# Hybrid Mamba-2 and attention layer on one core: operand splits get an edge behind the copies of turned blocks, and two half-size products change places

## The chip, the cores and the metric

One core of a Trainium2 chip runs the whole layer in one launch. The metric is device time in microseconds (us). The engines are TensorE (PE, with PEld for its weight loads), VectorE (DVE), ScalarE (ACT), GpSimd (POOL) and SyncE (SP, which here issues DMAs). ScalarE's queue issues DMAs too (ACTq).

## The reference

Input is x of 1024 x 1024, float32. One layer is computed:

```python
h = rmsnorm(x, pre_g)
proj = h @ w_in     # -> z_ssm | xBC | dt | q | k | v | f | z_att | g_ssm | g_att
# A: Mamba-2: causal conv and SiLU on xBC, chunked SSD scan, norm gated with silu(z_ssm)
# B: forgetting attention, 16 heads of 64: softmax(q k^T / 8 + F[t] - F[s]), causal,
#    F = cumsum(log_sigmoid(f)); output times silu(z_att)
merged = sigmoid(g_ssm) * (y_ssm @ w_branch_ssm) + sigmoid(g_att) * (y_att @ w_branch_att)
out = x + rmsnorm(merged @ w_out, post_g)
```

The result is compared with float32, so the kernel multiplies float32 values as sums of a high and a low part.

## The kernel before

**Products.** The projections are done in pairs of column blocks of 128 (`Pair`). A pair is a 2 x 2 block product done with seven half-size products instead of eight (Strassen's scheme), numbered 1 to 7. Each has an operand made of the weights (`a11`, `a12`, `a21`, `a22` or sums of them) and one made of the activations (`ops`). An operand is used as a high part, which ScalarE makes by a copy to a narrower type (`Pair.split`, L351, tile `wop`), and a low part, which VectorE makes as the difference (L352). A product is 12 matmuls of 128x512 in L130: four blocks of 128 rows times high x high, high x low, low x high. In the rows of the profile `x0h`, `x4h`, `x5h` are the activations' parts, so `x0` marks product 1, `x4` product 6, `x5` product 7.

Products 1, 6, 7 and 4 of a pair accumulate in one PSUM bank (`pb`), which ScalarE copies out between them (`keep`, L404); 5 and 3 accumulate in a second (`pc`), and 2 has a third. `give` (L412 to L418) adds what belongs together and hands it to the unit's handler, which applies gates and stores to DRAM.

**The stream.** `Stream.steps` is a list, written out by hand, of all products in the order in which TensorE runs them. `half()` issues half of the next product. With it, the operand of the product three steps ahead is prepared (`ahead`, `prepare`), and up to two splits of activations are made for pairs that use another operand set (`ops.some()`, L277 and L280). There are four `wop` tiles.

**Attention.** The loop at the end makes 48 visits (eight pairs of heads, six groups of query blocks each) and a last pass. A visit issues, in this order: the scores of two query blocks (`scores`: products into PSUM tiles `s`, then VectorE's addition of the bias and minimum at L1467, then ScalarE's exponential at L1471, tile `ex`); the weighted sums of the visit before (`weighted`, tile `av`); a number of halves of the stream (`ahead`); loads; the turning of the exponentials (`turned`: transposes on TensorE into tiles `pt`, copied to `p` by ScalarE at L1510, or by VectorE at L1508 for one block in four); and more halves (`behind`). `s` and `pt` share four PSUM banks, so that a copy `p<-pt` must end before the scores of the next visit can use its bank. Between `hold()` and `release()` the calls of `ops.some()` are put off to the next visit. `ends[4]` is the pair whose products run when the attention loop ends.

**Order.** A planner in the framework orders the instructions on each engine by priority and by dependences. What is traced in `tc.high_priority()` (the copies, `keep`, `give`, the exponentials) goes ahead of other work that is ready. `tc.issue_after(ins)` gives the instructions traced inside it an edge: on the engine of `ins` they come after it in the queue.

Of the kernel before, what the change touches and what calls it, by code (L numbers as in the profile page):

```python
# [11 lines left out]
AF = mybir.ActivationFunctionType  # L12
# [74 lines left out]
def hybrid_layer(ctx: ExitStack, tc, a, out):  # L87

    nc = tc.nc
# [42 lines left out]
    def turn(out_, in_, idn=ident):  # L132
        return tc.keep_in_program_order(nc.tensor.transpose(out_, in_, idn))  # L133
# [27 lines left out]
    class Operands:  # L161
# [9 lines left out]
        def __init__(self, name, src, there=lambda k, h: True, order=lambda op: op, queue=nc.gpsimd):  # L171
            self.src, self.there, self.order, self.queue = src, there, order, queue
            self.copy = src
            self.tiles, self.left, self.made, self.at, self.step = {}, {}, set(), {}, 0
            self.lows = {}
            self.dram = {n: tc.dram_tile([KH, P, HALF], F32, name=f"{n}_{name}") for n in self.LESS}
# [279 lines left out]
    class Stream:  # L456
# [6 lines left out]
        def __init__(self, pairs, double, last):  # L463
            self.pairs = pairs
            for n, p in enumerate(pairs):
                p.bank, p.other = (pj, "be"[n % 2]), (pjx, "d") if n < double else (pj, "c")

                p.between = n < double or n >= last

            p, q, r = pairs[0:3]  # L470
            self.steps = [(p, 1), (q, 1), (p, 2), (q, 2)] + [(p, n) for n in (6, 5, 7, 4, 3)]
            self.steps += [(q, 6), (q, 5), (q, 7), (r, 1), (q, 4), (q, 3)]
            for n in range(2, last):
                p, nxt = pairs[n], pairs[n + 1]
                self.steps += [(p, i) for i in ((2, 6, 5, 7) if n < double else (6, 2, 7, 5))] + [(nxt, 1)]
                self.steps += [(p, 4), (p, 3)] if n + 1 < last else [(p, 3), (p, 4)]

            a, b, c, d, e, f, g, h = pairs[last:]
            self.steps += [(a, 5), (a, 6), (a, 7), (b, 1), (a, 2), (a, 4), (a, 3)]
            for p, nxt in ((b, c), (c, d), (d, e)):  # L480
                self.steps += [(p, 2), (p, 6), (p, 5), (p, 7), (nxt, 1), (p, 4), (p, 3)]
            self.steps += [(f, 1), (e, 2), (e, 6), (e, 5), (e, 7), (f, 2), (e, 4), (e, 3)]
            self.steps += [(f, 6), (f, 5), (f, 7), (g, 1), (f, 4), (f, 3)]
            self.steps += [(g, 2), (g, 6), (g, 5), (g, 7), (h, 1), (g, 4), (g, 3)]
            self.steps += [(h, 6), (h, 5), (h, 7), (h, 2), (h, 3), (h, 4)]
            self.following = {p: n.ops for p, n in zip(pairs, pairs[1:]) if n.ops is not p.ops}
            self.building = []
            self.chores, self.line = [], []
            self.held = None
            self.count = 0  # L490
            self.at = 0
            self.run = None
            self.waiting = []
            self.loads = [(p, names) for p in pairs for names in (("a11", "a12"), ("a21", "a22"))]
            self.loaded = []
            self.load_next()
# [23 lines left out]
                self.prepare(p, which)  # L520

        def prepare(self, p, which):
            p.prepare(which)
            self.load_more()

        def after(self, halves, fn):

            self.waiting.append([halves, fn])

        def half(self):  # L530
            if self.run is None:
                if self.at == len(self.steps):
                    return False
                p, which = self.steps[self.at]
                if which == 7 and p.ops is ops_a and "merged" not in fin:
                    return False
                if p.ops is ops_a and not all(p.ops.ready(OPERAND[which].strip("-"), j) for j in range(KH)):
                    return False
                self.ahead(False)
                for ops in self.building:  # L540
                    ops.some(OPERAND[which])
                self.run = p.do(which)
                next(self.run)
            else:
                for _ in self.run:
                    pass
                self.run = None
                p, which = self.steps[self.at]
                if p in self.following:
                    ops = self.following[p]  # L550
                    if ops not in self.building:
                        self.building.append(ops)
                    ops.open(OPERAND[which])
                self.ahead(True)
                self.at += 1
            for ops in self.building:
                if self.held is None:
                    ops.some()
                else:
                    self.held.append(ops)  # L560
            for chores in (self.chores, self.line):
                if chores:
                    chore = chores.pop(0)
                    if chore:
                        chore()
            self.count += 1
            for w in self.waiting:
                w[0] -= 1
            for w in [w for w in self.waiting if w[0] <= 0]:
                self.waiting.remove(w)  # L570
                w[1]()
            return True
# [4 lines left out]

        def release(self):
            held, self.held = self.held or [], None
            for ops in held:  # L580
                ops.some()

        def do_chores(self):
            while self.chores:
# [550 lines left out]
    with tc.tile_pool(name="pro", bufs=1, reuse_waits="tile", side="right") as pro, tc.tile_pool(  # L1135
# [37 lines left out]
        def turned(tiles, k):  # L1173
            pt = prop.tile([P, HALF], F32, tag="pt", bufs=2, name="pt")
            for j in range(4):
                turn(pt[:, j * P : (j + 1) * P], tiles[j][:, k * P : (k + 1) * P]) 
            return pt
# [11 lines left out]
        stream = Stream(order + late + ends, len(order) + 3, len(order) + len(late) + 4)  # L1189
# [105 lines left out]
    with tc.tile_pool(name="att", bufs=1, reuse_waits="tile", side="right") as ap, tc.tile_pool(  # L1295
# [177 lines left out]
        def turned(hp, g, sent):  # L1473

            pair, h = GROUPS[g]
            bs = list(range(4 * h, min(4 * h + 4, pair[0] + 1)))
            made = {}  # L1480
            order = bs[-1:] + bs[:-1] if sent else bs
            tiles = {b: pp.tile([P, HALF], F32, tag="s", bufs=4, name="pt") for b in order}
            banks = {b: tiles[b].rearrange("p (e t c) -> p e t c", e=2, t=2) for b in order}

            def turn_one(b, e, t):
                turn(banks[b][:, e, t, :], ex[:, e, 1 - t, b % 4 * P : b % 4 * P + P])

            for e in range(2):
                for b in order:
                    turn_one(b, e, 1)  # L1490
            for b in order:
                bank, first = banks[b], max(b - pair[1], 0)
                if sent and b == bs[-1]:
                    assert first == 1
                    for hd, which in sent:
                        hd.turn(which, tiles[b])
                if not first:
                    for e in range(2):
                        turn_one(b, e, 0)
                if sent and b == bs[-1]:  # L1500
                    for hd, which in sent:
                        hd.send(which, tiles[b])
                p = ap.tile([P, 2, 2, P], F32, tag="p", bufs=4, name="p")
                to, src = (x[:, :, first:, :] for x in (p, bank))
                with tc.high_priority():

                    if b % 4 == 1 and hp < NK - 2:
                        nc.vector.tensor_copy(to, src)  # L1508
                    else:
                        nc.scalar.activation(to, src, AF.Copy)  # L1510
                made[b] = (hp, g, b, first, p)
            return [(*made[b], b == bs[0], b == bs[-1]) for b in bs]

# [116 lines left out]
        def room(m):  # L1630

            share = weights[m // 6] * rooms[m % 6] if m < 6 * NK - 1 else 1.4
            to = stream.steps.index((ends[4], 6))
            n = round((2 * (to - stream.at) - (stream.run is not None)) * share / left[0])
            left[0] -= share
            if m == 6 * NK - 1:
                return n // 2, n - n // 2
            behind = n // 2 if n > 3 else min(max(n - 1, 0), 1)
            return n - behind, behind

        made = []
        for m in range(6 * NK + 1):
# [9 lines left out]
            for hd, which in end(m - 1):  # L1652
                hd.free(which)
            if m == 6 * NK:
                stream.release()
                heads[NK - 1].out(2)
                break
# [9 lines left out]
            ahead, behind = room(m)  # L1667
# [82 lines left out]
```

## Time and profile before

| | us |
|---|---|
| median of the runs | 1289.23 |
| lowest of the runs | 1288.09 |
| profiled execution, its own time | 1288.76 |
| span of the profiled execution | 1287.0 |
| TensorE busy in it | 1253.9 |
| VectorE busy | 1010.0 |
| ScalarE busy | 794.7 |
| GpSimd busy | 259.8 |

The mean granted clock of TensorE was 0.997. The attention loop lies between about 690 and 1135 us from the start of the span; the projections of the merged branches and the output follow. A row of the timeline gives start, duration, engine, line, operation, output tile <- input tiles, shapes and count, and in brackets the idle time of the engine ahead of it with what ended it. A matmul's duration overlaps with the next one's, so the distance of two starts is the time that one takes from TensorE.

### The profile page before, as it was taken

Reading aid. Unit: us, or ns where it says so; the run is one execution under the profiler, and the core shown is the slowest. Engines: PE = TensorE matmul, PEld = TensorE weight load, DVE = VectorE, ACT = ScalarE, POOL = GpSimd, SP = SyncE. Lnnn points to the kernel's source line nnn. Section 1 sums busy time; section 2 is a strip of 40 time slices with the busy share of each in tenths; the row PEclk is TensorE's granted clock in tenths of the full one; section 3 lists DMA queues with packets and bytes.
Section 4 is the critical chain, followed back from the end, with each engine's and each line's share of the span. In section 5 each row is a group of like instructions: output and inputs, shape, how many; then the busy total and the mean of one; then the engine's idle time right before and its main releaser. Section 6 shows DMA issues by size and latency. Waiting matters only on the chain.

```text
span 1287.0 us, 20996 instructions
## 1 busy us (share of the span) xinstructions
PE 1253.9 (97%) x7054; PEld 987.4 (77%) x7054; DVE 1010.0 (78%) x1994; ACT 794.7 (62%) x1738; POOL 259.8 (20%) x250
## 2 busy tenths in 40 slices
PE   5999999999999999999999999999989999999997
PEld 4688888787888888878877777777767777778886
DVE  7988886987788978897767676767679666897976
ACT  7745665556665665566556666666667665753754
POOL 4000440013300330124101111211000111246052
PEclk9999999999999999999999999999999999999999
DMA  8232542646336533653356566665787656765932
GB/s 298 70 116 76 158 150 88 191 151 189 127 115 198 185 126 106 213 168 123 132 185 233 178 212 200 206 225 202 237 285 244 206 184 224 258 229 194 365 115 98
DMA packets 153515, 233.57 MB, mean 181 GB/s; under 512 B 15968, under 2 KB 61504, under 8 KB 153408
## 3 DMA queue, kind: packets, MB, share of 16 engines
q1 hardware_dynamic: 137408, 197.14, 47.4%
q10 hardware_dynamic: 11136, 19.11, 3.9%
q0 software_dynamic: 4864, 15.99, 3.2%
q8 instruction: 55, 0.90, 0.3%
q14 instruction: 52, 0.43, 0.1%
HBM read 162.99 MB, written 72.34 MB: 183 GB/s over the span
## 4 chain that ended last, share of the span: by engine, by line
PE 73%; DVE 9%; DMA 8%; ACT 5%; issue 3%; SPq 1%; POOL 0%; ACTq 0%; DVEq 0%; POOLq 0%
PE pb L130 30%; PE pc L130 17%; PE pd L130 6%; PE av L130 5%; PE s L130 5%; PE pt L133 5%; PE yps L130 2%; DVE wop L352 2%; DMA raw<-in_wu 1%; DVE sum L357 1%; DMA xt<-in_x 1%; PE st L130 1%; DVE xs L771 1%; PE tr L133 1%; ACT wop L351 1%
## 5 line engine op out<-in xcount | busy, mean ns | idle before, releaser
L352 DVE TENSOR_TENSOR wop<-sum,wop 128x512 fp32r<-128x512 f32 x180 | 138.6, 772 | 54.6 <-ACT wop L351 53.7
L351 ACT ACTIVATE wop<-sum 128x512 fp32r<-128x512 f32 x180 | 112.5, 626 | 111.5 <-DVE sum L357 52.8
L1471 ACT ACTIVATE ex<-ex,nm 128x512 f32<-128x512 f32 (+1 forms) x192 | 116.2, 606 | 71.8 <-DVE nm L1467 67.7
L404 ACT ACTIVATE s<-pb 128x512 f32<-128x512 f32 x144 | 85.1, 591 | 98.3 <-PE pb L130 95.3
L130 PE MATMUL pb<-x0h,wop 128*128 128x512 f32 x384 | 131.8, 400 | 0.0
L130 PE MATMUL pc<-x2h,wop 128*128 128x512 f32 x384 | 131.1, 400 | 0.3 <-DVE u L416 0.3
L130 PE MATMUL pc<-x3h,wop 128*128 128x512 f32 x384 | 129.8, 396 | 1.5 <-DVE th L414 1.2
L130 PE MATMUL pb<-x5h,wop 128*128 128x512 f32 x384 | 130.0, 395 | 1.0 <-ACT s L404 1.0
L130 PE MATMUL pb<-x6h,wop 128*128 128x512 f32 x384 | 129.5, 395 | 1.3 <-ACT s L404 1.3
L352 DVE TENSOR_TENSOR wop<-raw,wop 128x512 fp32r<-128x512 f32 x144 | 102.7, 714 | 34.4 <-ACT wop L351 33.7
L130 PE MATMUL pb<-x4h,wop 128*128 128x512 f32 x384 | 129.1, 395 | 0.0
L1467 DVE CUSTOM_DVE_ANT_0 ex<-s,fb 128x512 f32<-128x512 f32 (+1 forms) x192 | 96.9, 552 | 17.9 <-PE s L130 17.9
L351 ACT ACTIVATE wop<-raw 128x512 fp32r<-128x512 f32 x144 | 89.7, 623 | 13.1 <-PE pd L130 5.8
L130 PE MATMUL pd<-x1h,wop 128*128 128x512 f32 x288 | 96.3, 394 | 0.0
L130 PEld LDWEIGHTS pc<-x2h,wop 128*128 128x128 f32 x384 | 72.6, 189 | 18.0 <-issue 2.4
L130 PEld LDWEIGHTS pc<-x3h,wop 128*128 128x128 f32 x384 | 72.1, 188 | 18.7 <-DVE th L414 1.6
L130 PEld LDWEIGHTS pb<-x5h,wop 128*128 128x128 f32 x384 | 72.1, 188 | 18.6 <-ACT s L404 2.1
L130 PEld LDWEIGHTS pb<-x6h,wop 128*128 128x128 f32 x384 | 72.1, 188 | 18.5 <-issue 2.0
L130 PEld LDWEIGHTS pb<-x0h,wop 128*128 128x128 f32 x384 | 72.8, 189 | 17.6 <-issue 2.9
L130 PEld LDWEIGHTS pb<-x4h,wop 128*128 128x128 f32 x384 | 72.1, 188 | 16.7 <-issue 1.9
L133 PE MATMUL pt<-ident,ex 128*128 128x128 f32 x576 | 77.2, 277 | 5.2 <-ACT ex L1471 2.5
L133 PEld LDWEIGHTS pt<-ident,ex 128*128 128x128 f32 x576 | 67.4, 142 | 15.1 <-DVE nm L1467 4.3
(310 smaller groups left out, 2921.4 us busy)
## 6 DMA issues: line engine op xcount, KB each, us to landing
raw<-in_wu SPq DMA_DIRECT2D x128, 256.0 KB
csb<-cs_dram SPq DMA_DIRECT2D x32, 256.0 KB
fb<-f_dram SPq DMA_DIRECT2D x16, 512.0 KB
rb<-st_dram SPq DMA_DIRECT2D x48, 128.0 KB
wd<-in_wo SPq DMA_DIRECT2D x40, 128.0 KB
xt<-in_x SPq DMA_DIRECT2D x8, 512.0 KB
gs_dram<-th ACTq DMA_DIRECT2D x16, 256.0 KB
qh_dram<-th ACTq DMA_DIRECT2D x16, 256.0 KB
```

What stands on the lines that cost most here:

```text
L130: return tc.keep_in_program_order(nc.tensor.matmul(*args, **kw))
L133: return tc.keep_in_program_order(nc.tensor.transpose(out_, in_, idn))
L351: nc.scalar.activation(op[:, 0], src, AF.Copy)
L352: nc.vector.tensor_tensor(op[:, 1], src, op[:, 0], ALU.subtract)
L357: self.adds.tensor_tensor(t, x, y, ALU.add)
L404: nc.scalar.activation(s, ps, AF.Copy)
L771: nc.vector.scalar_tensor_tensor(d, u[:, o + j : o + j + HALF], cw[:, tile_idx, j : j + 1], d, ALU.mult, ALU.add)
L1467: nc.vector.tensor_tensor_reduce(o, s[e][:, 0:w], fb[hp, h][:, e, 0:w], 1.0, 3.0e38, ALU.add, ALU.min, nm)
L1471: pin(nc.scalar.activation(o, o, AF.Exp, scale=-1.0, bias=nm, accum_out=hd.at(hd.sm, i, h, e)))
```

## The change

Three things are edited. The stream remembers the last ScalarE copy of turned blocks (`front`). Whatever is prepared after it (the splits of weights in `prepare`, those of activations in `ops.some()`, both in the visit and when put off) is traced with an edge behind that copy, until the last pass sets `front` to None. In the steps of the pair `a = ends[4]`, product 7 and product 1 of the next pair change places. The held list now has callables in place of operand sets.

```diff
             a, b, c, d, e, f, g, h = pairs[last:]
-            self.steps += [(a, 5), (a, 6), (a, 7), (b, 1), (a, 2), (a, 4), (a, 3)]
+            self.steps += [(a, 5), (a, 6), (b, 1), (a, 7), (a, 2), (a, 4), (a, 3)]
...
+            self.front = None
...
         def prepare(self, p, which):
-            p.prepare(which)
+            with self.behind():
+                p.prepare(which)
             self.load_more()
+
+        def behind(self):
+
+            return nullcontext() if self.front is None else tc.issue_after(self.front)
...
             for ops in self.building:
                 if self.held is None:
-                    ops.some()
+                    with self.behind():
+                        ops.some()
                 else:
-                    self.held.append(ops)
+                    self.held.append(ops.some)
...
         def release(self):
             held, self.held = self.held or [], None
-            for ops in held:
-                ops.some()
+            for fn in held:
+                with self.behind():
+                    fn()
...
                     else:
-                        nc.scalar.activation(to, src, AF.Copy)
+                        copy = nc.scalar.activation(to, src, AF.Copy)
+                        stream.front = copy.ins
...
             if m == 6 * NK:
+                stream.front = None
                 stream.release()
```

In the built kernel the two programs have the same instructions. On ScalarE 23 high-part splits of weights stand behind copies of turned blocks that they stood ahead of before, 61 such places in all (one, three or four copies each), and a few splits of activations change places with exponentials. On VectorE the low parts of these follow to behind VectorE's own copy. On TensorE only the two products change places. On GpSimd one addition, and on SyncE a few weight loads, move by one to three places.

## The prediction

> **What bounds the kernel now.** I read the page's totals first, then the stretches around the attention loop, then what TensorE (PE) waited for there, and only then single stretches of the timeline.
>
> ```profile
> span 1287.0 us, 20996 instructions
> PE 1253.9 (97%) x7054; PEld 987.4 (77%) x7054; DVE 1010.0 (78%) x1994; ACT 794.7 (62%) x1738; POOL 259.8 (20%) x250
> ```
>
> TensorE is busy for 1253.9 of 1287.0 us, so all its idle time together is 33.1 us. The change adds and removes no instruction. It can only win idle time back, or make more of it. The next view cuts the span into stretches: in each row the length, then busy time of PE, PEld, DVE, ACT and POOL, the granted clock, the DMA share and GB/s.
>
> ```profile
> 690.00:955.00 265.00, 263.80 (x1845) 199.55 (x1845) 184.50 (x503) 174.09 (x442) 36.87 (x44) 1.00 0.63 209
> 955.00:960.00 5.00, 3.64 (x20) 2.48 (x18) 2.40 (x6) 3.06 (x6) 0.47 (x1) 1.00 0.97 330
> 960.00:965.00 5.00, 3.50 (x14) 2.72 (x15) 4.42 (x11) 4.37 (x13) 0.35 (x2) 0.57 0.98 354
> 965.00:970.00 5.00, 5.00 (x27) 3.46 (x27) 4.29 (x8) 3.95 (x9) 0.79 (x2) 0.75 0.77 293
> 1085.00:1090.00 5.00, 3.19 (x21) 2.31 (x21) 4.29 (x16) 3.71 (x10) 0.00 (x0) 1.00 0.64 198
> 1090.00:1135.00 45.00, 44.16 (x290) 32.90 (x289) 38.78 (x93) 34.99 (x87) 10.19 (x11) 1.00 0.69 234
> ```
>
> From 690 to 955 us the attention loop leaves TensorE idle for 1.2 of 265 us. Two short holes, near 957 and near 1087, hold most of the rest. What TensorE waited for from 690 to 1135 us (engine, line, what it waited for: total us, times, longest):
>
> ```profile
> PE pt L133 <- ACT ex L1471: 2.5, 2, 2.2
> PE pt L133 <- DVE nm L1467: 2.5, 4, 1.5
> PE s L130 <- ACT p L1510: 0.8, 2, 0.6
> PE pb L130 <- ACT s L404: 0.7, 1, 0.7
> PE s L130 <- DVE p L1508: 0.3, 1, 0.3
> ```
>
> These five sum to 6.8 us. The third and fifth, 1.1 us in three places, are waits of score products for the copies of turned blocks, which free the four banks tagged "s". That is what the new edges can touch. The fourth is the wait that the reordering touches. The first two are turnings that wait for the exponentials. Late exponentials are what this loop is sensitive to.
>
> **Part 1: the edges behind the copies.** The change adds an edge from the last ScalarE copy of a visit (`p<-pt`) to every split issued after it. In the built order 23 of the high-part splits of weights move behind copies, past 61 copies together. On VectorE the low part follows its high part, so it now comes after the visit's VectorE copy, directly ahead of the next score additions. What the moved pieces cost, from 690 to 1135 us (line, engine, operation, tiles, count | busy us, mean ns | idle before and its releaser):
>
> ```profile
> L1510 ACT ACTIVATE p<-pt 128x512 f32<-128x512 f32 x104 | 55.4, 587 | 14.9 <-PE pt L133 11.7 <-PE s L130 1.7 <-ACT st L1393 1.5
> L351 ACT ACTIVATE wop<-sum 128x512 fp32r<-128x512 f32 x34 | 21.3, 626 | 13.3 <-PE pc L130 13.1
> L352 DVE TENSOR_TENSOR wop<-sum,wop 128x512 fp32r<-128x512 f32 x34 | 23.9, 704 | 11.5 <-ACT wop L351 11.5
> ```
>
> A moved split of 626 ns lets the copies behind it end about 0.5 us earlier (the pitch, 744.30 to 744.82 in the next fence), and is itself later by the one to four copies that it passes, 0.6 to 2.3 us. A typical visit on ScalarE, then VectorE, then the product that this split feeds:
>
> ```profile
> 744.30 0.62 ACT L351 ACTIVATE wop<-sum 128x512 fp32r<-128x512 f32 x1
> 744.82 0.25 ACT L1393 ACTIVATE st<-pt 8x128 f32<-8x128 f32 x1
> 745.24 1.05 ACT L1510 ACTIVATE p<-pt 128x512 f32<-128x512 f32 x2
> 748.22 0.72 ACT L1471 ACTIVATE ex<-ex,nm 128x512 f32<-128x512 f32 x1 [1.93 <-DVE nm L1467]
> ...
> 744.95 0.69 DVE L352 TENSOR_TENSOR wop<-sum,wop 128x512 fp32r<-128x512 f32 x1 [1.62 <-ACT wop L351]
> 745.56 0.68 DVE L1508 COPY p<-pt 128x512 f32<-128x512 f32 x1
> 747.49 0.68 DVE L1467 CUSTOM_DVE_ANT_0 ex<-s,fb 128x512 f32<-128x512 f32 x1
> ...
> 762.35 0.48 PE L130 MATMUL pc<-x2h,wop 128*128 128x512 f32 x1
> ```
>
> The split and its low part are done at 744.95 + 0.69 = 745.64, and the product starts at 762.35, 16.7 us later, because operands are prepared three steps ahead. So up to 2.3 us of delay of a split costs its product **nothing**. The cover for the split itself is the 1.93 us in which ScalarE waits for the next score additions. Without that cover it would delay the exponentials by its pitch of 0.5 us.
>
> Do the earlier copies win anything? Only where TensorE waited for one, and the largest of these three waits was this:
>
> ```profile
> 944.84 0.29 ACTq L1394 DMA_DIRECT2D st_dram<-st  x1
> 945.18 0.60 ACT L1510 ACTIVATE p<-pt 128x512 f32<-128x512 f32 x1 [1.74 <-PE s L130]
> 945.83 0.55 PE L130 MATMUL s<-k,q 64*128 64x128 f32 x5 [0.63 <-ACT p L1510]
> ```
>
> The copy at 945.18 stands behind the issue of a store at 944.84, not behind a split; ScalarE was idle for 1.74 us ahead of it. Moving a split does not move it. I take 0 for the copies, with bounds of 0 and -1.1 us (all three waits gone).
>
> The other side is VectorE. The low part of 0.69 us now stands directly ahead of the score additions, and behind a split that is itself behind copies. VectorE waits for splits already:
>
> ```profile
> DVE wop L352 <- ACT wop L351: 36.0, 27, 2.8
> ```
>
> It waited 36.0 us in 27 places, and TensorE lost nothing measurable by it, since all its waits there are the 6.8 us above. In the visit shown, copies would end near 745.8, the split near 746.4, the low part near 747.1. The additions that started at 747.49 could still start at most a few tenths later. Where the exponentials have room that costs nothing; at the four turnings that already waited for `nm` (2.5 us) there is none. I take **+0.2 us**: one such turning of the four, delayed by a few tenths. The bounds are 0 and 4 x 0.69 = 2.8 us, a whole low part at each.
>
> **Part 2: the reordering.** The pair that ends the attention stream had its products 6 and 7 back to back, both accumulating in one bank, with the copy `keep` between them. After the change, product 1 of the next pair stands between.
>
> ```profile
> 1127.07 0.62 ACT L351 ACTIVATE wop<-raw 128x512 fp32r<-128x512 f32 x1
> 1133.96 0.60 ACT L404 ACTIVATE s<-pb 128x512 f32<-128x512 f32 x1 [1.32 <-PE pb L130]
> ...
> 1133.54 0.39 PE L130 MATMUL pb<-x4h,wop 128*128 128x512 f32 x1
> 1134.61 0.50 PE L130 MATMUL pb<-x5h,wop 128*128 128x512 f32 x1 [0.69 <-ACT s L404]
> 1137.23 0.39 PE L130 MATMUL pb<-x5h,wop 128*128 128x512 f32 x1
> 1137.46 0.39 PE L130 MATMUL pb<-x0h,wop 128*128 128x512 f32 x1
> ```
>
> From product 6 (x4) to product 7 (x5) the starts are 1134.61 - 1133.54 = 1.07 us apart; from product 7 to product 1 of the next pair (x0), which has another bank, 0.23 us. With product 1 between, the copy of 0.60 us runs under a product of 1137.23 + 0.23 - 1134.61 = 2.85 us, and 1.07 - 0.23 = **0.84 us** is saved. The high part of product 1's operand is done at 1127.07 + 0.62 = 1127.69, 6 us ahead of that product's new start. After the change product 2 alone stands between product 7's copy and product 4, again 2.85 us of cover for 0.60. If that cover were gone, the 0.84 would come back there. Bounds: 0 and -0.84.
>
> **What stays.** The largest hole of the loop:
>
> ```profile
> 956.57 0.33 ACTq L622 DMA_DIRECT2D ga_dram<-th  x1
> 956.94 1.16 ACT L280 ACTIVATE x1h<-x1l 128x512 fp32r<-128x512 f32 x2 [4.47 <-DMA fb<-f_dram]
> 960.89 0.69 PE L133 MATMUL pt<-ident,ex 128*128 128x128 f32 x2 [2.25 <-ACT ex L1471]
> 962.19 1.81 PE L133 MATMUL pt<-ident,ex 128*128 128x128 f32 x6 [0.61 <-DVE nm L1467]
> ```
>
> ScalarE stood for 4.47 us at a store's issue until the load of `fb` had landed; everything behind it waited, the exponentials came late, and TensorE was idle for 2.25 + 0.61 us. Then the clock was 0.57 and 0.75 for two stretches of 5 us: 5 x 0.43 + 5 x 0.25 = 3.4 us more. The change leaves the order of this store and this load as it is, so I keep the hole of 2.9 + 3.4 us.
>
> The Trainium skill (TensorE: Matmul & The Clock Gate, Part 1: The HAM clock gate) says that the clock halves after an idle window of about 3.4 us and returns after one busy window, and that the window runs free of the program. This trace agrees with half: 2.25 + 0.61 us of idling, with two short transposes between, sufficed here, and 1.8 us near 1087 (5.00 - 3.19) left the clock at 1.00. By the rule one window at half rate would cost an estimated 1.7 us, not 3.4, and by its free phase the same hole could cost either in another execution.
>
> **The sum**, against the profiled execution of 1288.76 us (span 1287.0 and 1.76 around it): 1288.76 - 0.84 + 0 + 0.2 = **1288.1 us**. The runs of before had a median of 1289.23 and a lowest of 1288.09, so this is no more than their spread.
>
> **Rivals.**
>
> *The copies and the large hole go too.* All waits for copies vanish (-1.1), and the new order lets the store's issue near 956 fall behind the load's landing, so that the hole of 2.9 and the slow clock of 3.4 us go: 1288.76 - 0.84 - 1.1 - 2.9 - 3.4 = 1280.5. For it: a shift of a few us in the splits there would do. Against it: 4.47 us of waiting is far more than the 0.6 to 2.3 us that a split moves.
>
> *Slower: the low parts hold up the score additions.* Place: VectorE's queue between a visit's copy and its L1467, where a late split now stops what is behind it. Price: at the four turnings without room 4 x 0.69 = 2.8 us, so 1288.1 - 0.2 + 2.8 = 1290.7; and if one of these holes reaches the 2.9 us that the clock paid for near 960, another 3.4, so 1294.1. It decides from the point where the delay is larger than the room of a visit's exponentials. For it: the 36.0 us that VectorE already waits for splits, and the four waits for `nm`. Against it: those 36.0 us cost TensorE next to nothing so far, and 23 moved splits are few among 48 visits.
>
> The Trainium skill (TensorE: Matmul & The Clock Gate, the paragraph on engine queue depths) calls the queues of ScalarE and VectorE strictly first in, first out, which speaks against an edge on an engine that has other work behind it. The 4.47 us above agree.
>
> *The change does nothing.* The splits were never on the path, and the seam's 0.84 us turns into another wait, for the copy ahead of product 4 or for the next pair's sums on GpSimd: 1288.8. For it: the wait for `L404` is one of 0.7 us in a stretch of 445.
>
> **How the numbers follow.** The forecast has a chance of 0.57 with its own range of 1286.5 to 1289.5 (the bounds -1.1 for the copies and +1 for the additions and the runs' spread). The first rival has 0.12, the slower one 0.18, no effect 0.13. The range of 1283.0 to 1293.0 leaves out the far ends of the first two rivals. Two per cent, 26 us, is about what a measurement of this kernel can tell from no change. All of TensorE's idle time is 33.1 us, and that of the loop 6.8, so a gain of 26 is hardly there, and a loss of 26 needs four more holes like that of 957, at 2.9 + 3.4 = 6.3 us each. Chances: faster 0.02, same 0.95, slower 0.03.
>
> **What would show it.** Right: the waits of TensorE from 690 to 1135 us still sum to 6 to 7 us, the wait for `s L404` at the seam is gone, the product of x0 runs ahead of that of x5 with 0.23 us between starts, ScalarE's wait of over 4 us near 957 stays with the clock below 1.00 behind it, and the splits of 744 stand behind the copies. Wrong: rows of `pt <- nm` or `pt <- ex` that grow past 5 us, a granted clock below 1.00 in a stretch other than 960 to 970, or the hole near 957 gone.

## The result, and the profile after

The changed kernel is slower. Its median is 1291.68 us against 1286.52 us for the kernel before; the ratio is 1.0039 with a 95% interval of 1.0029 to 1.0048, so +5.0 us by the ratio (3.7 to 6.2). Two runs of the kernel before, of 2074.61 and 2505.29 us, count as slow, and the ratio leaves them out. The forecast was 1288.1, 0.7 below the profiled execution of before. That execution, 1288.76, lay 2.2 above the median of all runs of its kernel.

The page's totals of the changed kernel, then TensorE's waits in the attention loop (690 to 1135 us) and behind it (1132 us to the end):

```profile
span 1290.0 us, 20981 instructions
PE 1255.2 (97%) x7054; PEld 987.7 (77%) x7054; DVE 1005.9 (78%) x1994; ACT 794.9 (62%) x1738; POOL 258.6 (20%) x250
...
PE pt L133 <- DVE nm L1475: 2.8, 4, 1.5
PE pt L133 <- ACT ex L1479: 1.7, 4, 0.8
PE s L130 <- DVE p L1516: 0.9, 1, 0.9
PE s L130 <- ACT p L1518: 0.4, 2, 0.2
...
PE pb L130 <- ACT s L404: 3.1, 1, 3.1
```

The four waits in the loop sum to 5.8 us; without the seam's 0.7 those of before summed to 6.1. The loop did not get worse by its waits. The engines' counts of instructions are those of before. The last row is new: the wait of 0.7 for `s L404` has become one of 3.1, at another place. The stretch at the seam by the window view, two rows of before, then two of after with one of the attention loop ahead of them (columns as in the prediction):

```profile
1140.00:1145.00 5.00, 5.00 (x24) 4.14 (x23) 5.00 (x9) 1.95 (x4) 3.51 (x3) 1.00 0.29 94
1145.00:1150.00 5.00, 5.00 (x24) 4.14 (x23) 4.43 (x5) 1.12 (x2) 4.37 (x4) 1.00 0.73 244
```

```profile
1085.00:1090.00 5.00, 4.72 (x20) 3.90 (x21) 3.69 (x14) 4.13 (x10) 1.08 (x2) 0.66 0.38 138
...
1140.00:1145.00 5.00, 1.92 (x8) 1.29 (x7) 4.97 (x8) 1.23 (x2) 2.63 (x3) 0.91 0.20 69
1145.00:1150.00 5.00, 5.00 (x18) 3.98 (x17) 2.12 (x3) 1.12 (x2) 4.05 (x3) 0.75 0.61 194
```

Before, TensorE was full at the seam at a clock of 1.00. After, it was busy for 1.92 of 5 us, and the clock was 0.91 in that stretch and 0.75 in the next, which costs 5 x 0.09 + 5 x 0.25 = 1.7 us more. The row from 1085 to 1090 shows one more slow stretch, 5 x 0.34 = 1.7 us, where before the clock was 1.00. The timeline of TensorE, ScalarE, VectorE and GpSimd shows what happens at the seam (the matmul at 1140.86 is the last of product 2, that at 1144.32 the first of product 4):

```profile
1132.70 0.39 PE L130 MATMUL pb<-x4h,wop 128*128 128x512 f32 x1
1132.92 0.39 PE L130 MATMUL pb<-x0h,wop 128*128 128x512 f32 x1
1140.86 0.39 PE L130 MATMUL pd<-x1h,wop 128*128 128x512 f32 x1
1144.32 0.80 PE L130 MATMUL pb<-x6h,wop 128*128 128x512 f32 x1 [3.08 <-ACT s L404]
...
1135.84 0.60 ACT L404 ACTIVATE s<-pb 128x512 f32<-128x512 f32 x1
1138.62 0.63 ACT L351 ACTIVATE wop<-raw 128x512 fp32r<-128x512 f32 x1 [0.62 <-PE pb L130]
1142.52 0.63 ACT L351 ACTIVATE wop<-sum 128x512 fp32r<-128x512 f32 x1 [3.27 <-POOL sum L357]
1143.67 0.60 ACT L404 ACTIVATE s<-pb 128x512 f32<-128x512 f32 x1 [0.52 <-DVE merged L414]
...
1141.29 1.74 DVE L352 TENSOR_TENSOR wop<-raw,wop 128x512 fp32r<-128x512 f32 x1
1142.96 0.68 DVE L414 TENSOR_TENSOR merged<-pd,s 128x512 f32<-128x512 f32 x1
...
1140.91 1.58 POOL L357 TENSOR_TENSOR sum<-sum,raw 128x512 f32<-128x512 f32 x1 [2.50 <-DVE wop L352]
```

The seam itself does what was forecast: from x4 to x0 the starts are 0.22 us apart in place of 1.07, and the forecast 0.84 us is won. But the copy after product 7 (L404 at 1143.67), which could start when product 7 ends (near 1138.6: the split at 1138.62 is released by it), starts 5 us later. Product 4 (x6), which accumulates in the same bank, waits for it. Two things hold the copy. It waited last for `merged L414`, the addition that uses up the kept copy of product 1. The kept copies live in **three buffers** of tag `s` (`keep`, bufs=3). In the new order the copies of (a,1), (a,6) and (b,1) are all alive when (a,7) wants a fourth. The first one free is that of (a,1), after product 2 and L414. And the planner put ahead of it in ScalarE's queue the split of 1142.52, which waits 3.27 us for a sum of GpSimd; perhaps it takes the copy to be late, but why it chose this order is not shown.

The profile of before already has these buffers at their limit:

```profile
1141.92 0.60 ACT L404 ACTIVATE s<-pb 128x512 f32<-128x512 f32 x1 [0.91 <-DVE merged L416]
```

There the copy of (b,1) waits 0.91 us for L416, the addition that uses up the copy of (a,7). TensorE did not idle for it, as its row from 1140 to 1145 shows, so the wait is easily passed over; but it says that a fourth copy has no place.

### The profile page after: what moved, and what is told of

The parts are those of the page before. It is cut to its first block, busy times and chain, and to the rows that moved or that the text cites. A ratio compares the mean times of both kernels' runs of the same rounds, so it can differ in the third digit from the quotient of the medians.

```text
span 1290.0 us, 20981 instructions
## 1 busy us (share of the span) xinstructions
PE 1255.2 (97%) x7054; PEld 987.7 (77%) x7054; DVE 1005.9 (78%) x1994; ACT 794.9 (62%) x1738; POOL 258.6 (20%) x250
## 4 chain that ended last, share of the span: by engine, by line
PE 74%; DVE 10%; DMA 7%; ACT 5%; issue 3%; SPq 1%; ACTq 0%; DVEq 0%; POOL 0%
PE pb L130 31%; PE pc L130 18%; PE pd L130 5%; PE av L130 5%; PE pt L133 5%; PE s L130 4%; PE yps L130 2%; DVE wop L352 2%; DVE sum L357 1%; DMA fb<-f_dram 1%; DMA raw<-in_wu 1%; DMA xt<-in_x 1%; DVE ex L1475 1%; PE tr_v L133 1%; PE st L130 1%
## 5 line engine op out<-in xcount | busy, mean ns | idle before, releaser
L352 DVE TENSOR_TENSOR wop<-sum,wop 128x512 fp32r<-128x512 f32 x180 | 135.3, 753 | 60.9 <-ACT wop L351 59.9
L404 ACT ACTIVATE s<-pb 128x512 f32<-128x512 f32 x144 | 85.1, 591 | 94.2 <-PE pb L130 92.7
```

Source lines behind the costliest of these rows:

```text
L352: nc.vector.tensor_tensor(op[:, 1], src, op[:, 0], ALU.subtract)
L404: nc.scalar.activation(s, ps, AF.Copy)
```

## The experiments

Theory A: the loss comes from the wait for a fourth kept tile, and the idle time drags the clock down. Theory B: the edges behind the copies make the loop's exponentials late. Theory C: the copy is late by its place in ScalarE's queue only. Each run is compared with the kernel before on the same chip.

**1 and 2: the change in two halves.**

```diff
-            self.steps += [(a, 5), (a, 6), (a, 7), (b, 1), (a, 2), (a, 4), (a, 3)]
+            self.steps += [(a, 5), (a, 6), (b, 1), (a, 7), (a, 2), (a, 4), (a, 3)]
```

> Only the exchange of products 7 and 1, without the edges. Theory A (the three buffers of tag s: at the seam a fourth kept tile is wanted, so that the copy after product 7 waits until product 2's result has been added): the whole loss is here, about +5 us against the kernel before, with a wait of 2.5 to 3.5 us of pb for s L404 after product 2 and a granted clock below 1.00 behind it. Theory B (the edges: low parts ahead of the score additions make exponentials late): this kernel is 0 to 0.8 us faster than before.

> Only the edges behind the copies, with the old order of the products. Theory A: within 1 us of the kernel before, TensorE's waits from 690 to 1135 us at 5 to 8 us as before. Theory B: +4 to +6 us, the wait of the turnings for nm or ex grown.

The exchange alone: 1289.23 against 1286.23, ratio 1.0024 (1.0010 to 1.0039), +3.1 us. The edges alone: 1287.73, ratio 1.0011 (0.9999 to 1.0023). The exchange costs something; the edges probably do, but their interval takes in 1. Theory A's expectation that the whole loss is in the exchange misses. Theory B falls as the main cause: its +4 us did not come, and the turnings' waits for `nm` and `ex` are 3.1 us in run 2's profile, against 5.0 before. The exchange alone, in its rows:

```profile
1131.73 5.79 POOL L357 TENSOR_TENSOR sum<-raw 128x512 f32<-128x512 f32 x1 [6.63 <-DMA th<-ga_dram]
1137.20 0.69 DVE L414 TENSOR_TENSOR merged<-pd,s 128x512 f32<-128x512 f32 x1 [0.81 <-PE pd L130]
1138.90 0.63 ACT L351 ACTIVATE wop<-sum 128x512 fp32r<-128x512 f32 x1 [3.78 <-POOL sum L357]
1139.43 0.58 ACT L404 ACTIVATE s<-pb 128x512 f32<-128x512 f32 x1
1140.07 0.50 PE L130 MATMUL pb<-x6h,wop 128*128 128x512 f32 x1 [2.91 <-ACT s L404]
...
1140.00:1145.00 5.00, 4.93 (x22) 4.08 (x23) 4.46 (x4) 1.13 (x3) 3.36 (x3) 1.00 0.74 243
```

The wait is here without any edge. The slow clock that was expected behind it is not in this profile, which is of the fastest of the 12 runs (1286.07). Over the 12 the mean granted clock was 0.9957 against 0.9970 for the kernel before, an estimated 0.0013 x 1287 = 1.7 us. In this execution the tile was free at 1137.20 + 0.69 = 1137.89, and the copy still had to pass the split of 1138.90. So the queue of theory C is a second lock on the same copy: whichever opens last ends the wait.

**3 and 4: one lock and both.** Run 3 gives the copy after product 7 a buffer of its own, and with it the planner puts the copy ahead of the split. Run 4 keeps three buffers and only moves the split.

```diff
-        def keep(self, ps):
-            s = wp.tile([P, HALF], F32, tag="s", bufs=3, name="s")
+        def keep(self, ps, pool=None):
+            s = (pool or wp).tile([P, HALF], F32, tag="sp" if pool else "s", bufs=1 if pool else 3, name="s")
...
-                    self.k7 = self.keep(self.b)
+                    self.k7 = self.keep(self.b, fin["pool"] if self is ends[4] else None)
```

```diff
-            urgent = tc.high_priority() if self.keys[0][0] == "merged" else nullcontext()
+            urgent = tc.high_priority() if self.keys[0][0] == "merged" else tc.issue_after(ends[4].kept) if self is ends[5] and which == 6 else nullcontext()
```

> The changed kernel, but the copy after product 7 of the pair that ends the attention goes to a tile of its own, so that no buffer is awaited. Theory A: the wait for s L404 after product 2 (3.1 us) is gone, no slow clock behind it, and the time falls to about 1286, within 1 us of before or below it. Theory B: no change, about 1291.7. Theory C (the copy is late because it stands in ScalarE's queue behind a split that waits 3.3 us for a sum of GpSimd): also about 1286, since the built order puts the copy ahead of that split here.

> The changed kernel with three buffers as it is, but the split that waits for GpSimd's sum gets an edge behind the copy after product 7, so that ScalarE's order at the seam is that of the kernel with a fourth tile. Theory A: the copy still waits for the addition L414 after product 2, the wait of 3.1 us of pb for s L404 stays (2.5 to 3.5), the time stays at about 1291.7. Theory C: the wait is gone and the time about 1286.

Run 3: 1286.54, ratio 1.0004 (0.9993 to 1.0016). Run 4: 1288.22, ratio 1.0010 (0.9996 to 1.0023). The copy of run 3, then VectorE, ScalarE, TensorE and the window behind of run 4:

```profile
1139.93 0.58 ACT L404 ACTIVATE s<-pb 128x512 f32<-128x512 f32 x1
```

```profile
1141.05 0.68 DVE L414 TENSOR_TENSOR merged<-pd,s 128x512 f32<-128x512 f32 x1
1141.76 0.60 ACT L404 ACTIVATE s<-pb 128x512 f32<-128x512 f32 x1 [4.16 <-DVE merged L414]
1142.41 0.50 PE L130 MATMUL pb<-x6h,wop 128*128 128x512 f32 x1 [2.82 <-ACT s L404]
...
1145.00:1150.00 5.00, 5.00 (x23) 4.14 (x23) 3.85 (x4) 1.12 (x2) 4.37 (x4) 1.00 0.57 193
```

With the fourth buffer nothing waits for `s L404` any more and the seam's loss is gone, as theories A and C both expect. Run 4 tells them apart. With the queue alone put right, ScalarE stands idle for 4.16 us until L414 and TensorE for 2.82: the buffer is enough to make the wait, and theory C falls as the sole cause. But the time of run 4 was not the 1291.7 expected. In its profile the clock stayed at 1.00 behind the wait, which explains 1.7 us of the difference of 3.5. Over its 12 runs the mean granted clock was 0.9971, against 0.9970 for the kernel before: over the runs this wait drew no slow clock. Run 5 gives an estimate of what the clock costs the changed kernel; why a wait only a little shorter escapes it stays open.

**5 and 6: the clock's part.** The changed kernel again, and with 12 matmuls more ahead of product 4, into a bank that nobody reads:

```diff
-        def matmuls(self, ps, which, x, first):
+        def matmuls(self, ps, which, x, first, fill=0):
+            f = fill and fin["bank"].tile([P, HALF], F32, tag="f", bufs=1, name="fill")
...
+            [mm(f, op[:, 0, n % KH, :], xh[:, n % KH, :], start=True, stop=True, skip_group_check=True) for n in range(fill)]
```

> The changed kernel as it is, beside the others of this group on one chip. Theory A: again about 5 us over the kernel before (3.5 to 6), made of a wait of about 3 us at product 4 less the 0.84 us won, and of a lower granted clock for the rest (the mean of the runs 0.995 against 0.997).

> The changed kernel with 12 matmuls more into a bank of their own ahead of product 4 of the pair that ends the attention, whose result nobody reads. They take about 2.8 us, all within the wait of 3.1 us, so that the wait stays in place and only TensorE's idling goes. Theory A with the clock as the second half of the loss: the mean clock goes back to about 0.997 and the time falls by 2 to 2.5 us, to about 1289. If the clock has no part in it: no change, 1291.7.

The changed kernel: 1290.58 against 1285.29, ratio 1.0043 (1.0029 to 1.0057). Its mean granted clock was 0.9955 against 0.9979, an estimated 0.0024 x 1288 = 3.1 us for all slow stretches together, most of what run 4 fell short of its expectation by. Its wait was 3.45 us in the profile, with 0.94 and 0.72 as the clock of the stretches at and behind it (the first row is the hole near 957):

```profile
960.00:965.00 5.00, 4.59 (x19) 3.68 (x20) 4.31 (x10) 4.62 (x12) 0.64 (x2) 0.66 1.00 352
...
1140.00:1145.00 5.00, 1.55 (x6) 1.21 (x6) 4.93 (x7) 1.23 (x2) 3.45 (x3) 0.94 0.32 106
1145.00:1150.00 5.00, 5.00 (x18) 3.97 (x16) 2.05 (x3) 1.12 (x2) 3.65 (x4) 0.72 0.57 191
```

Filled: 1289.32, ratio 1.0028 (1.0014 to 1.0041). TensorE in the filled kernel, and the window behind:

```profile
1140.61 2.88 PE L130 MATMUL fill<-x6h,wop 128*128 128x512 f32 x12
1144.57 0.50 PE L130 MATMUL pb<-x6h,wop 128*128 128x512 f32 x1 [1.08 <-ACT s L404]
...
1145.00:1150.00 5.00, 5.00 (x24) 4.12 (x23) 4.37 (x5) 1.12 (x2) 3.11 (x4) 1.00 0.55 192
```

Product 4 starts as late as in the changed kernel, but TensorE idles for 1.08 us in place of 3.08 and 3.45, and the clock stays at 1.00. Over the runs the mean granted clock rose from 0.9955 (6 runs) to 0.9973 (8 runs). The medians differ by 1.3 us, not the 2 to 2.5 expected, and the intervals overlap: the direction is as expected and the slow clock of 1.7 us is shown in the profiles, its share in the median only roughly.

**7 and 8: another exchange.** Product 2 between 6 and 7, so that three buffers suffice; without the edges and with them.

```diff
-            self.steps += [(a, 5), (a, 6), (a, 7), (b, 1), (a, 2), (a, 4), (a, 3)]
+            self.steps += [(a, 5), (a, 6), (a, 2), (a, 7), (b, 1), (a, 4), (a, 3)]
```

> The kernel before, without edges, with the steps (a,5), (a,6), (a,2), (a,7), (b,1), (a,4), (a,3): product 2 stands between 6 and 7, so that its addition frees a kept tile before the copy after 7 wants one. Theory A: neither the wait of 0.69 us after product 6 nor one of 3 us, the time 0 to 1.5 us below the kernel before. If any exchange at this place costs time by the loads and sums that it moves: 1 us or more above it.

> The same order of the products with the edges of the change. Against the kernel with this order alone it shows the edges' price a second time: theory A says within 1 us of it; theory B (late exponentials) 1.5 us or more above it, and the waits for nm or ex from 690 to 1135 us above 6 us.

Theory A misses the time of run 7, and what came is the other case named there, 1 us or more above: ratios of 1.0037 (1.0025 to 1.0049) and 1.0058 (1.0044 to 1.0071). In run 7, ScalarE, VectorE and TensorE:

```profile
1134.74 0.63 ACT L280 ACTIVATE x1h<-zr 128x512 fp32r<-128x512 f32 x1 [0.91 <-DVE zr L1425]
1134.02 0.69 DVE L1425 TENSOR_TENSOR zr<-o,rb 128x512 f32<-128x512 f32 x1 [0.41 <-DMA rb<-st_dram]
1137.04 0.68 DVE L281 TENSOR_TENSOR x1l<-zr,x1h 128x512 fp32r<-128x512 f32 x1
1135.43 0.50 PE L130 MATMUL pd<-x1h,wop 128*128 128x512 f32 x1 [2.27 <-ACT x1h L280]
1137.77 0.80 PE L130 MATMUL pd<-x1l,wop 128*128 128x512 f32 x1 [1.84 <-DVE x1l L281]
```

The kept-tile waits are gone as theory A says, but product 2 takes the activations `x1`, whose last block is made of the last heads' output (`zr`, which waits for a load of `rb`). Moved ahead, it waits 2.27 + 1.84 us, and the clock is 0.77 and 0.89 in the stretches from 1135 and 1140. In the old order 7 and (b,1) ahead of 2 give the attention's last result time to arrive. Run 8's waits at this place, 1.25 and 1.71, are shorter than those of run 7, and yet it is slower by 2.6 us in the medians. Its mean granted clock was 0.9947 against 0.9964, an estimated 0.0017 x 1290 = 2.2 us, and the two intervals overlap: the pair does not tell the edges' price. The turnings' waits for `nm` and `ex`, 4.8 us in its profile against 4.0 in run 7's, stay below theory B's 6.

**9: the exchange with a fourth tile, without the edges** (the two diffs of runs 1 and 3).

> The kernel before with the exchange of products 7 and 1 and a tile of its own for the copy after 7, without the edges. Theory A: neither the wait of 0.69 us after product 6 nor that of 3 us; the time 0 to 1.5 us below the kernel before, and below the changed kernel by 4 to 6 us, which makes it the fastest here.

1284.61 against 1286.24, ratio 0.9986 (0.9976 to 0.9997): -1.8 us by the ratio, the fastest here, a little more than the 1.5 expected at most, and clear of no change. ScalarE's copy and product 4:

```profile
1136.12 0.58 ACT L404 ACTIVATE s<-pb 128x512 f32<-128x512 f32 x1
1137.43 0.39 PE L130 MATMUL pb<-x6h,wop 128*128 128x512 f32 x1
```

The copy ends 0.7 us ahead of product 4, and TensorE's idling is nil there. The 0.84 us forecast for the seam lies within the interval (0.4 to 3.1 us).

**10, 11, 12: where the edges cost.** The edges alone again, only for the first seven pairs of heads, and only for the last pair:

```diff
-                        stream.front = copy.ins
+                        stream.front = copy.ins if hp < NK - 1 else None
```

```diff
-                        stream.front = copy.ins
+                        stream.front = copy.ins if hp == NK - 1 else None
```

> The edges alone, beside the next two, which hold them in two parts. The first look gave a ratio of 1.0011 with an interval that touches 1. If the edges cost something, again 1 to 2 us above the kernel before; if not, within 0.5 us.

> The edges only in the first seven pairs of heads, so that the order near the seam is that of the kernel before. Theory B (late exponentials in the loop): the whole price of the edges is here, 1 to 2 us. Theory D (the edges cost in the seam, by the sums of GpSimd and the loads that they put back there): within 0.5 us of the kernel before.

> The edges only in the last pair of heads. Theory D: the price of the edges is here, 1 to 2 us, and a wait of some 0.5 us at product 4 of the pair that ends the attention as in the first look. Theory B: within 0.5 us of the kernel before.

Ratios of 1.0010 (0.9999 to 1.0022), 1.0014 (1.0002 to 1.0026) and 0.9998 (0.9987 to 1.0008). In the first seven pairs of heads the edges cost about 1.8 us (0.3 to 3.3); in the last pair alone nothing clear of noise (-1.7 to 1.0), so theory D falls for the whole price. Theory B has the place right, but its mechanism does not show: the turnings' waits for `nm` and `ex` are 4.8 us in run 11's profile, 5.0 before. But the wait that theory D names is there. TensorE in run 12, in product 4:

```profile
1141.43 0.50 PE L130 MATMUL pb<-x6l,wop 128*128 128x512 f32 x1 [0.73 <-DVE x6l L281]
```

The low part of the activations comes late. The same wait is 0.57 us in run 2 and 0.72 in run 10, and is missing without these edges (before, run 11). In the changed kernel it does not show, as product 4 starts late for another reason there. The price in the first seven pairs has a row for one part of it. VectorE and TensorE near 988 us, of the kernel before and then of run 11:

```profile
987.68 0.42 DVE L1508 COPY p<-pt 128x256 f32<-128x256 f32 x1
988.02 0.68 DVE L1062 SCALAR_TENSOR_TENSOR th<-th 128x512 f32<-128x512 f32 x1
988.16 0.96 PE L130 MATMUL s<-k,q 64*128 64x512 f32 x5 [0.32 <-DVE p L1508]
```

```profile
986.77 0.68 DVE L1070 SCALAR_TENSOR_TENSOR th<-th 128x512 f32<-128x512 f32 x1
987.98 0.41 DVE L1516 COPY p<-pt 128x256 f32<-128x256 f32 x1
988.45 0.96 PE L130 MATMUL s<-k,q 64*128 64x512 f32 x5 [0.92 <-DVE p L1516]
```

The new order puts a gate of 0.68 us (the same line, numbered 8 higher) ahead of the copy that the scores wait for, and the wait grows from 0.32 to 0.92. The profiles of all kernels with the edges in these heads have this 0.9, those without them 0.3. The rest of the edges' price there, about 1 us, has no row that tells it from the spread of single profiles, and stays open.

## Why the prediction was right or wrong

**The seam (-0.84 taken, bounds 0 and -0.84): the step that failed.** Its gain is there, 0.84 us at 1132.92, and run 9, which has it without the new wait, is faster by 1.8 us (0.4 to 3.1). What failed is the sentence that product 2 gives "again 2.85 us of cover for 0.60". It asked how long the copy takes and not when it may start. Counting the kept tiles alive, four for three buffers, would have told that the copy has to wait until product 2 is over and its sum added, so that no product is left to cover it. The bound 0 should have been above 0: the addition of 0.68 and the copy of 0.60 stand bare on TensorE's path, 1.3 us against the 0.84 won, and what is queued ahead of both comes on top. Measured: 3.08 - 0.84 = +2.2 us.

**The slow clock was reckoned with at the wrong place.** The prediction kept 3.4 us for the hole near 957 and none at the seam, as no hole was expected there. The hole behind product 2 cost 1.7 us more. With the edges' 1.5 us (run 2: 1287.73 - 1286.23; run 10 gives 1.6) the terms make 2.2 + 1.7 + 1.5 = 5.4 us, against the 5.0 measured. That they agree so well is in part luck: 0.6 to 0.7 us of the edges' price is the wait of product 4, which the changed kernel does not have, and the 1.7 us come from one profile, while slow stretches elsewhere change from one execution to the next.

**The edges (+0.2 taken, bounds 0 and 2.8).** The size, about 1.5 us (clear of nothing in run 11, not in runs 2 and 10), lies within the bounds but far from the value taken. The mechanism forecast for a loss, the low parts ahead of the score additions, does not show: the waits of turnings for `nm` and `ex` were 5.0 us before and 4.5 after. What shows is a gate that passed VectorE's copy, worth 0.6 us, and in the last pair a late low part. The prediction looked at what is moved by the edges, and not at what takes the free place.

**The copies (0 taken).** Right: the waits for ScalarE's copies went from 0.8 to 0.4 us (1.0 in run 2), and the wait for VectorE's rose from 0.3 to 0.9.

**The hole near 957 (kept).** Here the one profile was given too much weight. In the profile of the changed kernel ScalarE waited 2.68 us for `fb` instead of 4.47, and the clock stayed at 1.00; in run 5, the same program, it was 0.66 from 960 to 965 us, as its row above shows. The hole is in every profile, its price changes from one execution to the next, and the prediction's 1288.76 held an expensive one. The prediction said itself that the same hole could cost either in another execution, and kept the 3.4 us all the same. Of its signs of being wrong one came: a clock below 1.00 elsewhere, at the seam and near 1087.

**The rivals.** "The change does nothing" named the right place, a wait "for the copy ahead of product 4", but priced it at 0.84, what it gives back, in place of what it can cost. The slower rival had the sign and a price of the right order at a wrong place. The range of 1283.0 to 1293.0 took in the median of 1291.68, but by luck: its upper end was made for the slower rival, whose mechanism does not show. And the limit of two per cent that the prediction gave for what can be measured was far too wide, as the interval of the change is 2.5 us wide.

## What to carry to other kernels

When two products or stages change places, count the buffers alive at every point of the new order, not only the cover in time: a copy that may not start has no use for cover. A copy that already waits for a buffer in the old profile, on or off the path, says that there is none to spare. The order that a planner makes can carry such a wait on: here it put other waiting work ahead of the copy, and behind it once the copy had a buffer. And a move of one instruction is a move of all that fills its place.

## What the runs showed of the hardware

Much the same hole had a slow clock behind it or not. Idle times of 3.08 and 3.45 us at the seam were followed by stretches at 0.91 and 0.75, and 0.94 and 0.72; those of 2.91 (run 1), 2.82 (run 4) and 1.08 us (run 6) by 1.00. The Trainium skill (TensorE: Matmul & The Clock Gate, Part 1: The HAM clock gate) has half rate after an idle window of about 3.4 us and one busy window to return, an estimated loss of 1.7 us. The size agrees, 5 x 0.09 + 5 x 0.25 = 1.7 us, and the other slow stretches have it too: over each of the fourteen profiles, up to 1280 us, what the 5-us stretches below 1.00 lose sums to 0, 1.7, 3.4 or 5.1 us, to within 0.1. The condition does not agree: 3.08 us of idling was enough at the seam, and 1.49 + 0.28 us near 1085 in the changed kernel's profile, while 1.46 + 0.28 us at the same place before left the clock at 1.00.

Additions of GpSimd and VectorE stretched each other: VectorE's low part took 1.74 us at 1141.29, under GpSimd's addition of 1140.91, against 0.69 elsewhere. In run 1 GpSimd's addition took 5.79 us, against 1.28 to 1.74 for the same form (`sum<-raw`) in the profile of before: it began beside eight operations of VectorE in a row, from 1131.49 to 1136.38, and ended 1.14 us after the last. The Trainium skill (SBUF — State Buffer, SBUF: two separate sides) says that the two share a port pair which one of them holds for a whole instruction, VectorE where it has two operands in SBUF. The rows agree: L414, with one operand in PSUM, took its usual 0.68 us at 1144.06 before, all of it beside a GpSimd addition from 1143.63 to 1145.29. In the changed kernel the stretched low part puts one more microsecond ahead of the addition that frees the buffer.
